# Two layers of a hybrid decoder trunk: the second block's splits at the joins pinned behind both norms, low parts issued behind four rows of blocks, and the fourth split on VectorE

## The chip, the cores and the metric

The kernel runs on one core of one Trainium2 chip. The metric is the device time of one execution in microseconds (us). TensorE (PE) multiplies matrices, VectorE (DVE), ScalarE (ACT) and GpSimd (POOL) do the elementwise work, and SyncE's queue (SP) issues the loads of the weights.

## The reference

Two layers over x of 256 tokens by 1024 features, float32. Each layer is a feed-forward block, a mixer and a second feed-forward block:

```python
def swiglu(h, w_in, w_out):
    gate, up = jnp.split(h @ w_in, 2, axis=-1)
    return (jax.nn.silu(gate) * up) @ w_out
...
for l in range(DEPTH):
    x = x + 0.5 * swiglu(rms_norm(x, norm_gain[l, 0]), w_ffn_in[l, 0], w_ffn_out[l, 0])
    x = x + hybrid_mixer(rms_norm(x, norm_gain[l, 1]), ...)
    x = x + 0.5 * swiglu(rms_norm(x, norm_gain[l, 2]), w_ffn_in[l, 1], w_ffn_out[l, 1])
```

`w_ffn_in` is 1024 by 5632 for each block, `w_ffn_out` 2816 by 1024. The mixer projects the normalised x by `w_in` (8388 columns), runs four attention branches, gates them, sums them and projects by `w_out`.

## The kernel before

**Products in two parts.** A float32 operand is split into a high part, rounded to fp32r, and a low part, the rest. `split` (L180 to L197) does this for a block of weights of 128 by 1024: ACT casts the high part `whi` (L195), then DVE, or POOL where the caller says so, subtracts it for the low part `wlo` (L196). Tile buffer numbers tell the blocks apart: `whi_5274` and `wlo_5275` are the two parts of one block. A product of 128 rows is then three matmuls, high by high, high by low, low by high: `mm3` (L199 to L202) issues the three for one block of rows (128 of the 1024 summed over) before it goes to the next.

**Blocks.** The token rows are two blocks of 128, i = 0 and 1. A feed-forward block works through pairs of column blocks j = 0 to 10. `up_first` (L268 to L297) is the product of j = 0, taken before the norm's row factors are known: 48 matmuls of 256 columns for each i (two halves g, eight rows of blocks, three parts), so 96 in all; then ACT's silu (`sl`, L283), DVE's product `av` (L285), and TensorE's transposes of `av` (L292). `up` (L299 to L324) does the other pairs with `mm2`; its first matmuls stand behind the transposes of `av` on TensorE, which takes its instructions in order.

**Splits ahead of time.** `first(j)` (L254 to L266) loads the raw weights of block j and gives four splits as things to be called later: those of j = 0 (four, low parts on POOL in the blocks behind a join) and those of j = 1, the second block (four, on DVE). The list of eight is `todo`.

**Joins.** `join` (L367 to L403) writes down the change from one block to the next: the last products of the old block, then the norm of the new one. `main(i)` of `norm` transposes x on TensorE (L140), multiplies by the gain on DVE (`xg`, L143), casts the high part `h` on ACT (L144) and subtracts the low part `h` on DVE (L147). `stats(i)` squares and sums x on ACT (`junk`, L153), adds on DVE (`ms`, L156) and takes the power on POOL (`rt`, L158). What `join` writes between `with in_order()` and its end is pinned: on TensorE, ACT and DVE those instructions keep the written order. Everything outside is placed by a scheduler that orders instructions by its own estimate of when they can start. `early` says how many splits are called ahead of the pinned part: 4 where a feed-forward block ends (its successor is a mixer or a feed-forward block), 3 where a mixer ends (its successor is a feed-forward block). Then one more split is called behind `main(0)` and one behind `main(1)`; the rest are called in `up_first` behind the first `av` (L286 to L288), outside the pinned part. The mixer's first projection (`ps0`, L527 to L535) does the same with its own list.

So there are five joins: ffn to mixer and mixer to ffn in each layer, ffn to ffn between the layers.

Of the kernel before, what the change touches and what calls it, by code (L numbers as in the profile page):

```python
# [20 lines left out]
KC = 8  # L21
# [47 lines left out]
def tile_trunk(ctx: ExitStack, tc: tile.TileContext, a: dict, out: bass.AP):  # L69
    nc = tc.nc  # L70
# [109 lines left out]
    def split(src, slots=own, eng=None):  # L180


        k, m = src.shape[1], src.shape[2]
        key = min(slots, key=lambda k: used.get(k, 0))
        ht, lt = key[:2]
        used[key] = max(used.values(), default=0) + 1
        if ht == "whi":
            hi = hi_p.tile([128, 1024], F32R, name="whi", tag="whi")
            lo = lo_p.tile([128, 1024], F32R, name="wlo", tag="wlo")
        else:  # L190
            hi = wk.tile([128, 1024], F32R, name="whi", tag=ht, bufs=NB.get(ht, 1))
            lo = wk.tile([128, 1024], F32R, name="wlo", tag=lt, bufs=NB.get(lt, 1))
        hv = hi[:, :k * m].rearrange("p (k m) -> p k m", k=k)
        lv = lo[:, :k * m].rearrange("p (k m) -> p k m", k=k)
        nc.scalar.copy(hv, src)  # L195
        (eng or nc.vector).tensor_tensor(lv, src, f(hv), op=ALU.subtract)  # L196
        return hv, lv  # L197
# [6 lines left out]
    def mm2(ps, wh, wl, r2, start, stop):  # L204
# [4 lines left out]
        for p in reversed(parts) if stop else parts:  # L209
            p()  # L210

    pinned = (mybir.EngineType.PE, mybir.EngineType.Activation, mybir.EngineType.DVE)

    @contextmanager
# [16 lines left out]
    def ffn(l, s, nxt=None, aside=None):  # L231

        early = aside is not None
# [22 lines left out]
        def first(j):  # L256

            rv, w = load_up(j), []
            slots = wide if j or not s else ends

            def one(g, q):
                w.append(split(rv[g][:, 4 * q:4 * q + 4, :], slots, nc.gpsimd if j == 0 and (l or s) else None))

            def two(c, g):
                w.append(split(rv[g][:, :, c * 128:(c + 1) * 128], slots))
            return w, [lambda x=x, y=y: (two if j else one)(x, y) for x in range(2) for y in range(2)]  # L266

        def up_first(j, w):  # L268

            for c in range(2):  # L270
                act[2 * j + c] = pair_tile()
            for i in range(NT):
                t = slice(i * 128, (i + 1) * 128)
                ps = pm.tile([128, 2, T], F32, name="pm", tag="pm")
                for g in range(2):
                    for k in range(KC):
                        wh, wl = w[2 * g + k // 4]
                        mm3(ps[:, g, :], hh[:, k, t], hl[:, k, t], wh[:, k % 4, :], wl[:, k % 4, :],
                            k == 0, k == KC - 1)
                    if i == 0:  # L280
                        yield
                sl = wk.tile([128, T], F32, name="sl", tag="sl")
                nc.scalar.activation(out=sl[:], in_=ps[:, 0, :], func=AF.Silu, scale=rs[:, i:i + 1])  # L283
                av = wk.tile([128, T], F32, name="av", tag="av")
                nc.vector.scalar_tensor_tensor(out=av[:], in0=ps[:, 1, :], scalar=rs[:, i:i + 1], in1=sl[:],  # L285
                                               op0=ALU.mult, op1=ALU.mult)  # L286
                if j == i == 0:
                    while todo:  # L288
                        todo.pop(0)()
                pst = pt.tile([128, 4, 128], F32, name="pt", tag="pt")  # L290
                for c in range(2):
                    nc.tensor.transpose(pst[:, c, :], av[:, c * 128:(c + 1) * 128], ident[:])  # L292
                for c in range(2):
                    ah, al = act[2 * j + c]
                    nc.scalar.copy(ah[:, t], pst[:, c, :])
                    nc.vector.tensor_tensor(al[:, t], pst[:, c, :], f(ah[:, t]), op=ALU.subtract)
# [77 lines left out]
    def join(rows0, grow0, tail, grow1, nxt, early):  # L374


        if nxt is None:
            rows0()
            grow0()
            for t in tail:  # L380
                t()
            grow1()
            return
        block, l, n = nxt
        todo = next(block)
        for _ in range(early):
            todo.pop(0)()
        with in_order():
            rows0()
            grow0()  # L390
            main, stats, h = norm(l, n)
            tail[0]()
            main(0)
            todo.pop(0)()
            for t in tail[1:]:
                t()
            grow1()
            block.send(h)
            main(1)
            todo.pop(0)()  # L400
            stats(0)
            next(block)
            stats(1)  # L403

    bias = const.tile([128, NLINE, T], F32, name="bias")
    gT = const.tile([128, 96], F32, name="gT")
# [75 lines left out]
    def mixer(l, nxt):  # L482
# [44 lines left out]
        hh, hl = h2[:, 0], h2[:, 1]  # L527
        ps0 = tiles()
        for i in range(NT):
            for e in range(4):  # L530
                part(ps0[i], 512, i, e, w0[e])
                if i == 0 and e % 2:
                    yield
            if i == 0:
                while todo:  # L535
                    todo.pop(0)()
# [430 lines left out]
        w = []  # L967
# [91 lines left out]
```

## Time and profile before

| | |
|---|---|
| median of 3 runs | 1365.43 us (1365.39 to 1365.67) |
| profiled execution | 1365.53 us, span 1363.8 us, so 1.73 us outside the span |
| TensorE (PE) busy | 1345.9 us, 99% |
| DVE / ACT / POOL busy | 955.2 us (70%) / 682.5 us (50%) / 352.2 us (26%) |
| mean granted clock of TensorE | 0.999 |

Rows of a timeline give the start and the duration of an instruction (or of xN like ones that follow each other), the engine, the line and the operation; in brackets stands the idle time of the engine just before it and what ended it. Successive instructions of ACT and DVE overlap a little in the rows, and those of TensorE much more, so what an instruction takes up of its engine is read from one start to the next. Idle time of TensorE is what counts here; it is 1% of the span.

### The profile page before, as it was taken

What the parts mean: (1) busy time and instruction counts of PE and PEld (TensorE: products, weight loads), DVE (VectorE), ACT (ScalarE), POOL (GpSimd) and SP (SyncE); (2) the same over time, 40 slices, a digit from 0 to 9 for tenths busy, and PEclk for the clock granted to TensorE, in tenths of its full rate; (3) what the DMA queues carried; (4) which work ended last, traced back from release to release, by engine and by line L of the source; (5) the groups of instructions that cost most, each with busy time, mean ns of one, the idle gap of its engine ahead of it and who ended that gap; (6) DMA issues with size and microseconds to landing.
All of it is one profiled execution on the core that took longest, in us unless ns stands there. A gap on an engine that the chain in (4) does not pass through costs nothing.

```text
span 1363.8 us, 20927 instructions
## 1 busy us (share of the span) xinstructions
PE 1345.9 (99%) x8129; PEld 1187.9 (87%) x8129; DVE 955.2 (70%) x1560; ACT 682.5 (50%) x1020; POOL 352.2 (26%) x296
## 2 busy tenths in 40 slices
PE   9999999999999999999999999999999999999998
PEld 8888889879999988888898888898799999888887
DVE  7767756786786677666577666567868767776663
ACT  6445435655444555444364444356554445654441
POOL 0413232240031232322413322322300212232221
PEclk9999999999999999999999999999999999999999
DMA  9589634544443475555646555354534335665530
GB/s 355 176 197 289 213 119 140 180 139 153 148 137 107 136 247 171 200 186 187 202 138 215 186 185 201 97 180 150 170 124 156 124 104 176 222 208 186 186 124 31
DMA packets 171148, 233.35 MB, mean 171 GB/s; under 512 B 5206, under 2 KB 142106, under 8 KB 171034
## 3 DMA queue, kind: packets, MB, share of 16 engines
q1 hardware_dynamic: 169724, 231.55, 52.5%
q8 instruction: 64, 1.05, 0.3%
q10 hardware_dynamic: 1326, 0.48, 0.1%
q14 instruction: 34, 0.28, 0.1%
HBM read 230.93 MB, written 1.60 MB: 171 GB/s over the span
## 4 chain that ended last, share of the span: by engine, by line
PE 93%; DVE 3%; ACT 2%; issue 1%; POOL 1%; DVEq 0%; ACTq 0%
PE pt L207 11%; PE pm L207 11%; PE pm L200 6%; PE pm L202 6%; PE pm L201 6%; PE acc L201 6%; PE acc L202 6%; PE acc L200 6%; PE pt L208 6%; PE pm L208 5%; PE zp L201 5%; PE zp L202 4%; PE zp L200 4%; PE ov L622 2%; DVE wlo L196 2%; PE pt L616 1%
## 5 line engine op out<-in xcount | busy, mean ns | idle before, releaser
L195 ACT CAST whi<-raw 128x1024 fp32r<-128x1024 f32 (+5 forms) x446 | 452.6, 1020 | 426.9 <-PE pm L201 93.8
L196 DVE TENSOR_TENSOR wlo<-raw,whi 128x1024 fp32r<-128x1024 f32 (+3 forms) x426 | 512.3, 1207 | 156.4 <-ACT whi L195 154.8
L207 PE MATMUL pt<-h,whi 128*128 128x512 f32 x640 | 231.7, 397 | 0.4
L207 PE MATMUL pm<-h,whi 128*128 128x512 f32 x640 | 231.9, 396 | 0.0
L319 POOL TENSOR_TENSOR sl<-sl,rb 128x256 f32<-128x256 f32 x80 | 91.6, 1145 | 309.8 <-ACT sl L318 309.8
L208 PE MATMUL pt<-h,wlo 128*128 128x256 f32 x640 | 166.4, 280 | 0.0
L208 PE MATMUL pm<-h,wlo 128*128 128x256 f32 x640 | 166.2, 280 | 0.0
L200 PE MATMUL pm<-h,whi 128*128 128x256 f32 x512 | 147.0, 287 | 0.4 <-DVE tg L946 0.4
L202 PE MATMUL pm<-h,wlo 128*128 128x256 f32 x512 | 146.8, 287 | 0.0
L201 PE MATMUL pm<-h,whi 128*128 128x256 f32 x512 | 146.1, 285 | 0.0
L207 PEld LDWEIGHTS pm<-h,whi 128*128 128x128 f32 x640 | 120.1, 188 | 23.0 <-issue 0.6
L207 PEld LDWEIGHTS pt<-h,whi 128*128 128x128 f32 x640 | 120.1, 188 | 22.4 <-ACT rb L166 1.0
L201 PE MATMUL acc<-wlo,act 128*128 128x512 f32 x352 | 137.9, 393 | 0.1
L202 PE MATMUL acc<-whi,act 128*128 128x512 f32 x352 | 137.5, 392 | 0.0
L200 PE MATMUL acc<-whi,act 128*128 128x512 f32 x352 | 137.1, 393 | 0.0
L323 POOL TENSOR_TENSOR act<-av,act 128x256 fp32r<-128x256 f32 x80 | 96.1, 1201 | 155.3 <-ACT act L322 155.3
L208 PEld LDWEIGHTS pt<-h,wlo 128*128 128x128 f32 x640 | 120.8, 189 | 7.1
L208 PEld LDWEIGHTS pm<-h,wlo 128*128 128x128 f32 x640 | 120.7, 189 | 6.8
L201 PE MATMUL zp<-wlo,h 128*128 128x512 f32 (+4 forms) x320 | 115.8, 362 | 1.1 <-DVE wlo L196 1.1
L202 PE MATMUL zp<-whi,h 128*128 128x512 f32 (+4 forms) x320 | 114.8, 359 | 0.0
L200 PE MATMUL zp<-whi,h 128*128 128x512 f32 (+4 forms) x320 | 109.7, 363 | 1.2 <-ACT whi L195 1.2
L200 PEld LDWEIGHTS pm<-h,whi 128*128 128x128 f32 x512 | 97.9, 191 | 3.5 <-issue 3.4
(198 smaller groups left out, 2274.9 us busy)
## 6 DMA issues: line engine op xcount, KB each, us to landing
raw<-in_w_ffn_in_dram SPq DMA_DIRECT2D x66, 1024.0 KB
raw<-in_w_in_dram SPq DMA_DIRECT2D x52, 1024.0 KB
raw<-in_w_ffn_out_dram SPq DMA_DIRECT2D x44, 1024.0 KB
raw<-in_w_ffn_in_dram SPq DMA_DIRECT2D x44, 512.0 KB
raw<-in_w_branch_dram SPq DMA_DIRECT2D x8, 1024.0 KB
raw<-in_w_out_dram SPq DMA_DIRECT2D x8, 1024.0 KB
raw<-in_w_in_dram SPq DMA_DIRECT2D x8, 768.0 KB
raw<-in_w_in_dram SPq DMA_DIRECT2D x4, 840.0 KB
```

Source lines behind the costliest of these rows:

```text
L195: nc.scalar.copy(hv, src)
L196: (eng or nc.vector).tensor_tensor(lv, src, f(hv), op=ALU.subtract)
L200: nc.tensor.matmul(ps, lhsT=lh, rhs=rh, start=start, stop=False)
L201: nc.tensor.matmul(ps, lhsT=lh, rhs=rl, start=False, stop=False)
L202: nc.tensor.matmul(ps, lhsT=ll, rhs=rh, start=False, stop=stop)
L207: parts = [lambda: nc.tensor.matmul(ps, lhsT=wh, rhs=r2, start=start, stop=stop), lambda: nc.tensor.matmul(ps[:, 0], lhsT=wl, rhs=r2[:, 0] ...
L208: lambda: nc.tensor.matmul(ps[:, 0], lhsT=wl, rhs=r2[:, 0], start=False, stop=False)]
L319: nc.gpsimd.tensor_tensor(sl[:], sl[:], rb[:], op=ALU.mult)
L323: nc.gpsimd.tensor_tensor(al, av[:], f(ah), op=ALU.subtract)
L616: nc.tensor.transpose(pst[:, c, :], ps[j][:, b * 128:(b + 1) * 128], ident[:])
L622: nc.tensor.matmul(o[:, hs[j], :], lhsT=pT[:, c, :], rhs=pv(hs[j], b), start=b == 0, stop=b == nb - 1)
```

## The change

Three edits. `mm3_late` takes four rows of blocks at a time: for each of the four high by high and high by low, and behind them the four matmuls of low by high; `up_first` and the mixer's `ps0` use it. The fourth split of j = 0 of the feed-forward blocks behind a mixer gets its low part from DVE and no longer from POOL. In `join` the split behind `main(0)` is called only where `early` is 4, and all that is left of `todo` is called behind `stats(1)`, inside the pinned part.

```diff
--- before.py
+++ after.py
@@ -209,6 +209,15 @@
         for p in reversed(parts) if stop else parts:
             p()
 
+    def mm3_late(ps, ops, start, stop):
+
+        n = len(ops)
+        for j, (lh, ll, rh, rl) in enumerate(ops):
+            nc.tensor.matmul(ps, lhsT=lh, rhs=rh, start=start and j == 0, stop=False)
+            nc.tensor.matmul(ps, lhsT=lh, rhs=rl, start=False, stop=False)
+        for j, (lh, ll, rh, rl) in enumerate(ops):
+            nc.tensor.matmul(ps, lhsT=ll, rhs=rh, start=False, stop=stop and j == n - 1)
+
     pinned = (mybir.EngineType.PE, mybir.EngineType.Activation, mybir.EngineType.DVE)
 
     @contextmanager
@@ -259,7 +268,7 @@
             slots = wide if j or not s else ends
 
             def one(g, q):
-                w.append(split(rv[g][:, 4 * q:4 * q + 4, :], slots, nc.gpsimd if j == 0 and (l or s) else None))
+                w.append(split(rv[g][:, 4 * q:4 * q + 4, :], slots, nc.gpsimd if j == 0 and (l or s) and not (s and g == q == 1) else None))
 
             def two(c, g):
                 w.append(split(rv[g][:, :, c * 128:(c + 1) * 128], slots))
@@ -273,10 +282,10 @@
                 t = slice(i * 128, (i + 1) * 128)
                 ps = pm.tile([128, 2, T], F32, name="pm", tag="pm")
                 for g in range(2):
-                    for k in range(KC):
-                        wh, wl = w[2 * g + k // 4]
-                        mm3(ps[:, g, :], hh[:, k, t], hl[:, k, t], wh[:, k % 4, :], wl[:, k % 4, :],
-                            k == 0, k == KC - 1)
+                    for q in range(2):
+                        wh, wl = w[2 * g + q]
+                        mm3_late(ps[:, g, :], [(hh[:, 4 * q + k, t], hl[:, 4 * q + k, t], wh[:, k, :], wl[:, k, :])
+                                               for k in range(4)], q == 0, q == 1)
                     if i == 0:
                         yield
                 sl = wk.tile([128, T], F32, name="sl", tag="sl")
@@ -391,7 +400,8 @@
             main, stats, h = norm(l, n)
             tail[0]()
             main(0)
-            todo.pop(0)()
+            if early == 4:
+                todo.pop(0)()
             for t in tail[1:]:
                 t()
             grow1()
@@ -401,6 +411,8 @@
             stats(0)
             next(block)
             stats(1)
+            while todo:
+                todo.pop(0)()
 
     bias = const.tile([128, NLINE, T], F32, name="bias")
     gT = const.tile([128, 96], F32, name="gT")
@@ -527,9 +539,11 @@
         hh, hl = h2[:, 0], h2[:, 1]
         ps0 = tiles()
         for i in range(NT):
-            for e in range(4):
-                part(ps0[i], 512, i, e, w0[e])
-                if i == 0 and e % 2:
+            t = slice(i * 128, (i + 1) * 128)
+            for q in range(2):
+                mm3_late(ps0[i], [(hh[:, kk, t], hl[:, kk, t], w0[kk // 2][0][:, kk % 2, :], w0[kk // 2][1][:, kk % 2, :])
+                                  for kk in range(4 * q, 4 * q + 4)], q == 0, q == 1)
+                if i == 0:
                     yield
             if i == 0:
                 while todo:
```

Three places of the order, on ACT and DVE. In the changed kernel the lines behind `mm3_late` have other numbers: the silu is L292 there, `av` L294, its transposes L301.

First, ACT at the join from mixer to ffn in layer 0, before, from the last cast of `h` to the second silu. `whi_5278` is a split of the second block, whose other three stand further ahead; `whi_5517`, `whi_5538` and `whi_5572` are splits of block j = 2, which the scheduler placed.

```order
L144 CAST h2_5189<-xg_5273 128x4x128
L195 CAST whi_5278<-raw_5142 128x1024
L153 ACTIVATE junk_5283,ss_5282<-x_87 128x512
L153 ACTIVATE junk_5285,ss_5282<-x_87 128x512
L153 ACTIVATE junk_5315,ss_5314<-x_87 128x512
L153 ACTIVATE junk_5317,ss_5314<-x_87 128x512
L195 CAST whi_5517<-raw_5512 128x1024
L283 ACT_TABLE_LOAD
L283 ACTIVATE sl_5322<-pm_5235,rt_5190 128x256
L195 CAST whi_5538<-raw_5514 128x1024
L195 CAST whi_5572<-raw_5512 128x1024
L283 ACTIVATE sl_5394<-pm_5345,rt_5190 128x256
```

ACT at the same place now, from the third of the four squares to the first silu; `whi_5318`, `whi_5322`, `whi_5326` and `whi_5330` are the second block's splits.

```order
L153 ACTIVATE junk_5311,ss_5310<-x_87 128x512
L195 CAST whi_5517<-raw_5512 128x1024
L153 ACTIVATE junk_5313,ss_5310<-x_87 128x512
L195 CAST whi_5318<-raw_5142 128x1024
L195 CAST whi_5322<-raw_5144 128x1024
L195 CAST whi_5326<-raw_5142 128x1024
L195 CAST whi_5330<-raw_5144 128x1024
L195 CAST whi_5538<-raw_5514 128x1024
L195 CAST whi_5572<-raw_5512 128x1024
L292 ACT_TABLE_LOAD
L292 ACTIVATE sl_5334<-pm_5231,rt_5190 128x256
```

Ahead of the table load and the first silu stood one split behind the squares; now six stand there. DVE at this place before, from the low part of `whi_5278` to the first `av` and one row on:

```order
L196 TENSOR_TENSOR wlo_5279<-raw_5142,whi_5278 128x1024
L156 SCALAR_TENSOR_TENSOR ms_5287<-ss_5282 128x1
L156 SCALAR_TENSOR_TENSOR ms_5319<-ss_5314 128x1
L196 TENSOR_TENSOR wlo_5518<-raw_5512,whi_5517 128x1024
L285 SCALAR_TENSOR_TENSOR av_5324<-pm_5235,rt_5190,sl_5322 128x256
L196 TENSOR_TENSOR wlo_5539<-raw_5514,whi_5538 128x1024
```

DVE at this place now, from the low part of the fourth split of j = 0 (`wlo_5275`, which was POOL's) to the first `av`:

```order
L196 TENSOR_TENSOR wlo_5275<-raw_5140,whi_5274 128x1024
L156 SCALAR_TENSOR_TENSOR ms_5283<-ss_5278 128x1
L196 TENSOR_TENSOR wlo_5518<-raw_5512,whi_5517 128x1024
L156 SCALAR_TENSOR_TENSOR ms_5315<-ss_5310 128x1
L196 TENSOR_TENSOR wlo_5319<-raw_5142,whi_5318 128x1024
L196 TENSOR_TENSOR wlo_5323<-raw_5144,whi_5322 128x1024
L196 TENSOR_TENSOR wlo_5327<-raw_5142,whi_5326 128x1024
L196 TENSOR_TENSOR wlo_5331<-raw_5144,whi_5330 128x1024
L196 TENSOR_TENSOR wlo_5539<-raw_5514,whi_5538 128x1024
L196 TENSOR_TENSOR wlo_5573<-raw_5512,whi_5572 128x1024
L294 SCALAR_TENSOR_TENSOR av_5336<-pm_5231,rt_5190,sl_5334 128x256
```

Between the second `ms` and the first `av` stood one low part; now there are six.

Second, DVE some microseconds earlier in the same join, where the low parts `h2` of the first row block are made (L147), before:

```order
L147 TENSOR_TENSOR h2_5189<-xg_5203,h2_5189 128x4x128
L196 TENSOR_TENSOR wlo_5331<-raw_5142,whi_5330 128x1024
L147 TENSOR_TENSOR h2_5189<-xg_5211,h2_5189 128x4x128
L979 TENSOR_TENSOR x_87<-xo_5047,x_87 128x512
L196 TENSOR_TENSOR wlo_5327<-raw_5144,whi_5326 128x1024
L196 TENSOR_TENSOR wlo_5335<-raw_5144,whi_5334 128x1024
L143 TENSOR_TENSOR xg_5265<-pt_5260,gn_106 128x512
```

And now:

```order
L143 TENSOR_TENSOR xg_5211<-pt_5206,gn_106 128x512
L147 TENSOR_TENSOR h2_5189<-xg_5203,h2_5189 128x4x128
L147 TENSOR_TENSOR h2_5189<-xg_5211,h2_5189 128x4x128
L993 TENSOR_TENSOR x_87<-xo_5047,x_87 128x512
L143 TENSOR_TENSOR xg_5261<-pt_5256,gn_106 128x512
L143 TENSOR_TENSOR xg_5269<-pt_5264,gn_106 128x512
```

The three low parts of the second block that stood between and behind the two rows of L147 are gone from here.

Third, DVE at the join from ffn to ffn (layer 0 to layer 1), before, from the low part of the split behind `main(1)` to the first `av`:

```order
L196 TENSOR_TENSOR wlo_7011<-raw_6870,whi_7010 128x1024
L156 SCALAR_TENSOR_TENSOR ms_7019<-ss_7014 128x1
L156 SCALAR_TENSOR_TENSOR ms_7051<-ss_7046 128x1
L196 TENSOR_TENSOR wlo_7246<-raw_7240,whi_7245 128x1024
L285 SCALAR_TENSOR_TENSOR av_7056<-pm_6967,rt_6915,sl_7054 128x256
```

And now:

```order
L196 TENSOR_TENSOR wlo_7011<-raw_6870,whi_7010 128x1024
L156 SCALAR_TENSOR_TENSOR ms_7019<-ss_7014 128x1
L156 SCALAR_TENSOR_TENSOR ms_7051<-ss_7046 128x1
L196 TENSOR_TENSOR wlo_7055<-raw_6868,whi_7054 128x1024
L196 TENSOR_TENSOR wlo_7059<-raw_6870,whi_7058 128x1024
L196 TENSOR_TENSOR wlo_7246<-raw_7240,whi_7245 128x1024
L294 SCALAR_TENSOR_TENSOR av_7064<-pm_6967,rt_6915,sl_7062 128x256
```

Two low parts of the second block, which stood ahead of the norm of the second row block (as `wlo_7059` and `wlo_7063`, by the numbers of before), now stand as `wlo_7055` and `wlo_7059` between `ms` and `av`; on ACT their casts stand in the same way between the squares and the silu.

## Rows read from the trace of the kernel before

**Rows 1.** The page: busy time of the first engines; shares of the chain.

```profile
PE 1345.9 (99%) x8129; PEld 1187.9 (87%) x8129; DVE 955.2 (70%) x1560; ACT 682.5 (50%) x1020; POOL 352.2 (26%) x296
...
PE 93%; DVE 3%; ACT 2%; issue 1%; POOL 1%; DVEq 0%; ACTq 0%
```

**Rows 2.** TensorE's waits over the span: us in total, times, longest.

```profile
PE pm L202 <- DVE h L147: 3.0, 3, 1.2
PE pt L546 <- DVE zn L559: 2.4, 2, 1.2
...
PE pt L292 <- DVE av L285: 1.0, 2, 0.5
```

**Rows 3.** Timeline of TensorE, mixer to ffn join of layer 0.

```profile
496.63 0.28 PE L200 MATMUL pm<-whi,h 128*128 128x256 f32 x1
...
499.64 0.39 PE L202 MATMUL pm<-whi,h 128*128 128x256 f32 x1 [1.19 <-DVE h L147]
...
500.93 1.03 PE L140 MATMUL pt<-ident,x 128*128 128x128 f32 x8
...
510.30 0.28 PE L202 MATMUL pm<-whi,h 128*128 128x256 f32 x1
511.11 0.41 PE L292 MATMUL pt<-ident,av 128*128 128x128 f32 x2 [0.53 <-DVE av L285]
```

**Rows 4.** Timeline of ACT, same join.

```profile
503.09 1.22 ACT L144 CAST h<-xg 128x512 fp32r<-128x512 f32 x2 [5.16 <-DVE xg L143]
504.22 1.04 ACT L195 CAST whi<-raw 128x1024 fp32r<-128x1024 f32 x1
505.17 0.62 ACT L153 ACTIVATE junk<-x 128x512 f32<-128x512 f32 x1
...
507.63 1.03 ACT L195 CAST whi<-raw 128x1024 fp32r<-128x1024 f32 x1
508.68 1.28 ACT L283 ACT_TABLE_LOAD   x1
509.97 0.47 ACT L283 ACTIVATE sl<-pm,rt 128x256 f32<-128x256 f32 x1
```

**Rows 5.** Timeline of DVE, same join.

```profile
494.97 0.69 DVE L147 TENSOR_TENSOR h<-xg,h 128x512 fp32r<-128x512 f32 x1
...
496.72 2.87 DVE L147 TENSOR_TENSOR h<-xg,h 128x512 fp32r<-128x512 f32 x1
...
505.29 1.23 DVE L196 TENSOR_TENSOR wlo<-raw,whi 128x1024 fp32r<-128x1024 f32 x1 [0.25 <-ACT whi L195]
...
510.48 0.48 DVE L285 SCALAR_TENSOR_TENSOR av<-pm,rt,sl 128x256 f32<-128x256 f32 x1 [0.56 <-ACT sl L283]
511.41 2.36 DVE L196 TENSOR_TENSOR wlo<-raw,whi 128x1024 fp32r<-128x1024 f32 x2 [0.45 <-ACT whi L195]
```

**Rows 6.** Timeline of POOL, same join.

```profile
496.56 2.48 POOL L196 TENSOR_TENSOR wlo<-raw,whi 128x1024 fp32r<-128x1024 f32 x1 [3.47 <-ACT whi L195]
```

**Rows 7.** Timeline of SP, same join: loads of raw weights.

```profile
502.48 4.43 SPq L253 DMA_DIRECT2D raw<-in_w_ffn_in_dram  x2
```

**Rows 8.** Timeline of ACT, same join: first split from those loads of w_ffn_in.

```profile
517.47 1.05 ACT L195 CAST whi<-raw 128x1024 fp32r<-128x1024 f32 x1
```

**Rows 9.** Windows at the end: length; busy time by engine; PEclk, DMA share, GB/s.

```profile
1359.00:1360.00 1.00, 0.98 (x5) 0.46 (x3) 0.68 (x1) 0.00 (x0) 0.00 (x0) 1.00 0.00 0
...
1361.00:1362.00 1.00, 0.00 (x0) 0.00 (x0) 0.00 (x0) 0.00 (x0) 0.00 (x0) 1.00 1.00 375
1362.00:1363.00 1.00, 0.00 (x0) 0.00 (x0) 0.00 (x0) 0.00 (x0) 0.00 (x0) 0.51 0.28 107
```

**Rows 10.** Timeline of TensorE at the start: matmuls ahead of the first work.

```profile
1.05 5.49 PE L103 MATMUL idle<-ones 128*128 128x128 f32 x24 [1.05 <-DVE neg_half L114]
```

**Rows 11.** Timeline of DVE, ffn to ffn join: the first av.

```profile
697.51 0.48 DVE L285 SCALAR_TENSOR_TENSOR av<-pm,rt,sl 128x256 f32<-128x256 f32 x1
```

**Rows 12.** Timeline of TensorE, same join: the transposes of av.

```profile
698.85 0.38 PE L292 MATMUL pt<-ident,av 128*128 128x128 f32 x2
```

## The prediction

> **What bounds the kernel now.** I read the page first, then TensorE's waits, then the timelines of the engines at one join. The page shows TensorE busy for 1345.9 us, 99% of the span, and the chain of waits lies on it for 93% [rows 1]. So an edit can win only from TensorE's few waits, and it can lose wherever it makes a new one. The table of waits shows which lines lose time: the low parts of `h` at L202 (3.0 us in three waits, one in the start and one in each join from mixer to ffn), a norm in the mixer (L546, 2.4 us in two) and `av` at L292 (1.0 us in two) [rows 2]. The timelines show the two that this change touches, in the join from mixer to ffn of layer 0; the join of layer 1 repeats it. TensorE begins the new block's first product at 496.63, stops for the low part of `h` and goes on at 499.64; the matmul ahead of that gap starts at 498.18 by the same timeline, so the stop costs 1.46 less a usual step of 0.12, some 1.35. At the end of the product, its last matmul starts at 510.30, and the transposes of `av` start at 511.11: 0.69 lost [rows 3]. All matmuls of the next pair stand behind those transposes.
>
> **Part 1: what the moved splits remove.** The first stop has its cause in DVE's queue. The second low part of `h` took 2.87 us where the first took 0.69 [rows 5], and it lies beside POOL's low part of the fourth split, 496.56 to 499.04 [rows 6]. With that split on DVE, and with the second block's low parts gone from between the two, L147 needs 0.69 again and ends some 2 us before TensorE wants it. The gain is 1.35 in each join. Nothing of the old block moves, so the first product still begins at 496.63, and TensorE would be through with it at 510.30 + 0.12 - 1.35 = 509.07.
>
> **Part 2: what they put in the way.** ACT and DVE take their instructions in order, and in the pinned order the second block's four splits stand behind both norms, two more from the scheduler join them, and only then come the table load, the first silu and the first `av`. When does this queue start? The transposes of the second row block stand behind the first 24 matmuls, now at 496.63 + 24 x 0.12 = 499.5 where they were at 500.93 [rows 3]; `xg` follows some 0.6 behind the start, at 500.1. Before, DVE started it at 502.38 (its casts on ACT follow at 503.09 [rows 4]), so this norm comes 2.3 earlier. ACT then does: casts of `h` from 500.8; the fourth split's cast at 504.22 - 2.3 = 501.95; the squares 0.95 later (505.17 - 504.22), which take 507.63 - 505.17 = 2.46 as before, with one cast of 0.95 among them. So the six casts begin at 501.95 + 0.95 + 2.46 + 0.95 = 506.3 [rows 4]. DVE's low part starts 1.07 behind its cast (505.29 against 504.22), at 507.4. From start to start it needs 2.36 - 1.22 = 1.14 (two of them in 2.36, of which one is 1.22) [rows 5]. Six of them: 507.4 + 6.84 = 514.2, and then `av`. ACT alone would be sooner: 506.3 + 6 x 0.95 + 1.29 for the table load = 513.3 for the silu, and `av` 0.51 behind it (510.48 against 509.97) [rows 4, 5]. DVE is therefore the later. TensorE follows 0.63 behind `av`'s start (511.11 against 510.48), at 514.85. Before it was 511.11: **+3.75 a join, +7.5 for both**. This holds both removed waits already, since both times count from the same 496.63. TensorE now stands still from 509.07 to 514.85, 5.8 us.
>
> The other instructions that move: the loads behind these splits. A raw buffer is free when both splits of it are done, so SP's two loads at 502.48 [rows 7] wait for the third and fourth low part of the queue, to about 510 and 511, and the load of `w_ffn_out` ahead of them from 499.07 to about 504.3. The first split from the loads of `w_ffn_in` was cast at 517.47 [rows 8], now some 3.7 later at 521. That is 10 us behind the issue where it was 15; two of these loads were issued within 4.43 [rows 7]. I cost them at nothing. If that cover were gone, the wait would be the part of a load beyond 10 us, in both joins.
>
> **Part 3: the ffn to ffn join.** No wait was there: `av` began at 697.51, the transposes at 698.85, as soon as the product was through [rows 11, 12]. Two low parts of 1.14 now stand ahead of `av`: 697.51 + 2.28 = 699.8, plus 0.63 = 700.4, against 698.85: **+1.55**. In the two ffn to mixer joins two splits move in the same way, but there no `av` stands behind them, and the table of waits has none of TensorE's at these joins [rows 2]: 0, with a bound of two low parts, 2.3 a join, if they were wholly bare.
>
> **Part 4: low parts behind four rows.** Low by high is wanted eight matmuls later than before, 8 x 0.12 = 0.95. At the joins this is inside part 2. In the first block of the kernel it sets against the third wait of L202 (3.0 less two of 1.2, so 0.6) [rows 2]: I take **-0.5**, between 0 and -0.95. In the mixers the scheduler puts some transposes elsewhere, around the norm that L546 waits for: 0, between -2.4, if both its waits went [rows 2], and +2.1 for both, if in each eight transposes (1.03 [rows 3]) that used to run in the wait no longer do.
>
> **Part 5: the clock.** A stop of 5.8 us on TensorE is not in the trace, outside its two ends. At the end TensorE's last matmul is over before 1360.0; the granted clock is 1.00 in the window of 1361 to 1362 and 0.51, the lower level (1.2 GHz), in the next [rows 9]. So it fell about 2 us behind the last work. In the new stop that would come at 511 to 512, and TensorE would begin the second pair at half speed. How long it stays so no row shows. The bounds: nothing, if it does not fall; and half of 5.49 us, 2.75, if it takes as long to come back as the matmuls that the kernel runs ahead of its first work [rows 10]. I take 2.0 a join, nearer the upper end, since the stop is almost three times what the clock bore at the end: **+4.0**.
>
> The Trainium skill says on this ("TensorE: Matmul & The Clock Gate", Part 1) that half rate is the array's default state, that sustained matmul activity releases it, and that the clock goes back when the engine idles. By it the slow stretch comes in each of the two joins; by the rows of work alone, where the clock never fell between two matmuls, part 5 would be 0.
>
> **Sum.** 7.5 + 1.55 - 0.5 + 4.0 = 12.55. The profiled execution took 1365.53 (span 1363.8 and 1.73 around it), 0.10 above the median: 1378.1.
>
> **The rivals.**
> *The clock stays up.* For it: in the work of this trace it never fell. Against: the stop is longer than any there. Time: 1365.53 + 8.55 = 1374.1. Chance 0.22.
> *Half the queue.* If the six splits start about 2.5 us sooner than I have it, because `xg` is not held by TensorE's 24 matmuls, or if a low part costs less with POOL quiet, `av` waits for some 1.3 beyond before, TensorE stands still for 3 us, and the clock barely matters: 2 x 1.3 + 1.0 - 0.5 = 3, so 1368.6; with two more of the six covered, 1366. Against it: 1.14 was read where POOL had nothing to do. Chance 0.12.
> *The queue is through in time, and the change wins.* Only the removed waits would count: two times 1.35 + 0.69 = -4.1, and -0.5 at the start: 1360.9. It is decided where the sixth low part ends: it has to be before 508.4, that is 0.63 ahead of TensorE's end of the product at 509.07, so the six have to start at 501.6 and not at 507.4. For it speaks only that the casts of the fourth split are ready about then; against it the order, with the squares ahead of them on ACT. Chance 0.06.
> *The change does nothing that counts*, since each new wait is won back later by a TensorE that waited there anyway. Against: the page has no other waits of this size. 1365.5, chance 0.04.
>
> **How the numbers follow.** My forecast has 0.56. Two tenths of a per cent, 2.7 us, is about what a measurement of this kernel can tell from no change. Slower by more than that are the forecast, the rival with the clock up and most of the third case: 0.86. Within it: a part of the third and the last: 0.08. Faster: 0.06. The forecast's own bounds run from 1374 (clock price 0) to 1380 (2.75 each, and the mixers' +2.1 makes 1382). The range goes down to 1368.5, to take in most of the half queue, and up to 1383, for a load that comes late.
>
> **What would show it.** Right: no wait of L202 on `h` in the two joins; a wait of TensorE of 5 to 6 us on `av`, twice; the table load on ACT near 512; `av` right behind six low parts, near 514.2; a wait of 1 to 2 us at the same line in the ffn to ffn join; matmuls of twice the duration behind the long waits, with a granted clock of 0.5 for some microseconds. Wrong: TensorE's wait on `av` below 3 us, or a long wait on a raw load.

## The result, and the profile after

The changed kernel takes 1377.68 us (median of 5 runs, 1377.2 to 1378.88), the kernel before 1365.43 on the same chip: 1.0092 times as long, 95% interval 1.0081 to 1.0103. It is slower by 12.25 us. The profiled execution took 1377.68, its span is 1375.9.

TensorE's waits in the profile after (us in total, times, longest), to be held against [rows 2]:

```profile
PE pt L301 <- DVE av L294: 12.6, 3, 5.6
PE pt L560 <- DVE zn L573: 2.2, 2, 1.1
PE pm L201 <- DVE wlo L196: 1.5, 2, 0.8
```

The wait for the low part of `h` is gone from the list. In its place stands one line of 12.6 us: three waits for `av`. The join from mixer to ffn of layer 0, on ACT, DVE and TensorE, answers to [rows 3 to 5]. ACT, timeline of the changed kernel:

```profile
506.29 5.77 ACT L195 CAST whi<-raw 128x1024 fp32r<-128x1024 f32 x6
512.08 1.28 ACT L292 ACT_TABLE_LOAD   x1
513.37 0.84 ACT L292 ACTIVATE sl<-pm,rt 128x256 f32<-128x256 f32 x2
```

DVE, same window:

```profile
494.92 1.29 DVE L147 TENSOR_TENSOR h<-xg,h 128x512 fp32r<-128x512 f32 x2
496.78 0.69 DVE L993 TENSOR_TENSOR x<-xo,x 128x512 f32<-128x512 f32 x1 [0.57 <-PE xo L202]
500.08 1.29 DVE L143 TENSOR_TENSOR xg<-pt,gn 128x512 f32<-128x512 f32 x2 [2.61 <-PE pt L140]
...
507.36 6.90 DVE L196 TENSOR_TENSOR wlo<-raw,whi 128x1024 fp32r<-128x1024 f32 x6 [0.27 <-ACT whi L195]
514.18 0.87 DVE L294 SCALAR_TENSOR_TENSOR av<-pm,rt,sl 128x256 f32<-128x256 f32 x2
```

TensorE, same window:

```profile
508.45 0.64 PE L219 MATMUL pm<-whi,h 128*128 128x256 f32 x4
514.71 0.69 PE L301 MATMUL pt<-ident,av 128*128 128x128 f32 x2 [5.62 <-DVE av L294]
515.05 0.77 PE L207 MATMUL pm<-h,whi 128*128 128x512 f32 x1
```

The two low parts of `h` take 1.29 together where the second alone took 2.87. The six casts, the table load, the six low parts and `av` follow one another, and TensorE's transposes begin at 514.71. DVE stands still for 2.61 between its add and `xg`: that is where two of the second block's low parts ran before (the third stood between the two rows of `h`). The first matmul with 512 columns behind the wait takes 0.77. Its like before (timeline of TensorE):

```profile
511.27 0.48 PE L207 MATMUL pm<-h,whi 128*128 128x512 f32 x1
```

The windows of the changed kernel (length; busy by engine; PEclk, DMA share, GB/s) say why:

```profile
513.00:514.00 1.00, 0.00 (x0) 0.00 (x0) 1.00 (x2) 0.99 (x3) 0.00 (x0) 1.00 1.06 373
514.00:515.00 1.00, 0.29 (x2) 0.29 (x3) 1.00 (x3) 1.00 (x2) 0.00 (x0) 0.58 1.08 379
515.00:516.00 1.00, 1.00 (x5) 0.90 (x4) 0.87 (x2) 0.41 (x2) 0.00 (x0) 0.50 0.90 285
516.00:517.00 1.00, 1.00 (x5) 0.80 (x4) 0.80 (x3) 0.17 (x1) 0.00 (x0) 0.50 0.99 340
517.00:518.00 1.00, 1.00 (x6) 0.86 (x5) 0.29 (x1) 0.10 (x1) 0.00 (x0) 0.72 1.12 347
518.00:519.00 1.00, 1.00 (x8) 0.92 (x7) 0.00 (x0) 0.00 (x0) 0.00 (x0) 1.00 1.01 342
```

The granted clock is at its lower level, 1.2 GHz, from about 514.2 to 517.6.

**Where the 12.2 us came in.** Both programs issue 8129 matmuls, so the n-th of one trace can be held against the n-th of the other. The difference of their starts grows from stage to stage; what each stage adds, in us:

```
start of the kernel                     -0.36
mixer of layer 0                        +0.33
join mixer to ffn, layer 0              +4.38
join ffn to ffn                         +1.58
mixer of layer 1                        +1.27
join mixer to ffn, layer 1              +4.97
sum at the last matmul                 +12.18   (1359.59 -> 1371.77)
```

### The profile page after: what moved, and what is told of

Its sections match the earlier page's. It is cut to its first block, busy times and chain, and to the rows that moved or that the text cites. A ratio compares the mean times of both kernels' runs of the same rounds, so it can differ in the third digit from the quotient of the medians.

```text
span 1375.9 us, 20928 instructions
## 1 busy us (share of the span) xinstructions
PE 1349.3 (98%) x8129; PEld 1191.7 (87%) x8129; DVE 953.9 (69%) x1562; ACT 680.8 (49%) x1020; POOL 346.0 (25%) x294
## 4 chain that ended last, share of the span: by engine, by line
PE 94%; DVE 3%; ACT 2%; issue 1%; DMA 0%; POOL 0%; SPq 0%; ACTq 0%; DVEq 0%
PE pm L207 11%; PE pt L207 11%; PE acc L200 6%; PE acc L201 6%; PE acc L202 6%; PE pm L200 6%; PE pm L208 6%; PE pt L208 5%; PE pm L201 5%; PE pm L202 5%; PE zp L201 4%; PE zp L202 4%; PE zp L200 4%; PE ov L636 2%; DVE wlo L196 2%; PE pt L630 1%
## 5 line engine op out<-in xcount | busy, mean ns | idle before, releaser
L207 PE MATMUL pm<-h,whi 128*128 128x512 f32 x640 | 234.8, 400 | 0.0
L207 PE MATMUL pt<-h,whi 128*128 128x512 f32 x640 | 231.6, 396 | 0.5 <-ACT rb L166 0.4
L200 PE MATMUL pm<-h,whi 128*128 128x256 f32 x512 | 147.0, 287 | 0.4 <-DVE tg L960 0.4
L202 PE MATMUL pm<-h,wlo 128*128 128x256 f32 x512 | 146.8, 287 | 0.0
L207 PEld LDWEIGHTS pm<-h,whi 128*128 128x128 f32 x640 | 121.6, 190 | 23.5 <-issue 0.6
L207 PEld LDWEIGHTS pt<-h,whi 128*128 128x128 f32 x640 | 120.1, 188 | 22.5 <-ACT rb L166 0.9
L202 PE MATMUL acc<-whi,act 128*128 128x512 f32 x352 | 137.5, 392 | 0.0
L200 PE MATMUL acc<-whi,act 128*128 128x512 f32 x352 | 137.2, 394 | 0.0
L201 PE MATMUL zp<-wlo,h 128*128 128x512 f32 (+4 forms) x288 | 102.8, 357 | 1.1 <-DVE wlo L196 1.1
L202 PE MATMUL zp<-whi,h 128*128 128x512 f32 (+4 forms) x288 | 102.2, 355 | 0.0
L200 PEld LDWEIGHTS pm<-h,whi 128*128 128x128 f32 x512 | 97.9, 191 | 3.5 <-issue 3.4
L320 DVE TENSOR_TENSOR z<-pt,sl 128x512 f32<-128x512 f32 x80 | 55.3, 692 | 64.5 <-POOL sl L328 62.8
```

The lines of the kernel that those rows point to most:

```text
L200: nc.tensor.matmul(ps, lhsT=lh, rhs=rh, start=start, stop=False)
L201: nc.tensor.matmul(ps, lhsT=lh, rhs=rl, start=False, stop=False)
L202: nc.tensor.matmul(ps, lhsT=ll, rhs=rh, start=False, stop=stop)
L207: parts = [lambda: nc.tensor.matmul(ps, lhsT=wh, rhs=r2, start=start, stop=stop), lambda: nc.tensor.matmul(ps[:, 0], lhsT=wl, rhs=r2[:, 0] ...
L320: nc.vector.tensor_tensor(z[:], ps[g][:], by[:].rearrange("p (o t) -> p o t", o=1) .to_broadcast([128, 2, T]), op=ALU.mult)
```

## The experiments

My theory: the low parts pinned behind both norms form one queue ahead of `av`; they leave a stretch in which DVE is free, and the stop that they make drops TensorE's clock. Rivals: one of the other two edits (the order of the low parts; POOL's split given to DVE) is the cause, or the pinning itself is, whatever the queue's length. Each ratio is to the kernel before on the same chip, whose median lay between 1365.38 and 1365.52. What a stage adds is read as in the table above, from n-th against n-th matmul of the profiled execution.

**One edit alone: the order of the low parts.** Only `mm3_late` and its two users:

```diff
-                        mm3(ps[:, g, :], hh[:, k, t], hl[:, k, t], wh[:, k % 4, :], wl[:, k % 4, :],
-                            k == 0, k == KC - 1)
+                        mm3_late(ps[:, g, :], [...], q == 0, q == 1)
```

> The kernel before with mm3_late alone. If the queue of splits ahead of av is the cause of the loss: start -0.4, mixers +0.3 and +1.3 as in the changed kernel, and nothing at the mixer to ffn joins, because the stop for the low part of h shrinks by 0.95 but av still comes at about 510.5: 1366.6 us. If the new order of the low parts is itself the cause: near 1377.

Measured: 1365.85 us, ratio 1.0004 (0.9995 to 1.0013), no difference that can be told. The stop for the low part of `h` shrinks to two of 0.5 (waits: `PE pm L219 <- DVE h L147` 1.0 in two), and TensorE then waits longer for `av` (2.5 in two), as expected: what the first wait gives, the second takes. This edit is not the cause.

**One edit alone: the pinned calls.**

```diff
             next(block)
             stats(1)
+            while todo:
+                todo.pop(0)()
```

> The kernel before with the second block's splits called behind stats(1) in the pinned part, alone. If the queue is the cause: four low parts stand between the norms and av in place of six, and the fourth split of j = 0 is out of that queue (POOL has it), so av starts at 511.0 and the transposes at 511.6 (+0.5 a join), the stop for the low part of h is gone, and the ffn to ffn join loses 1.6: 1368.0 us. If calling them there is by itself the whole cause: 1376 or more.

Measured: 1371.09 us, ratio 1.0041 (1.0028 to 1.0053). The queue was as computed (timeline of DVE):

```profile
506.32 4.63 DVE L196 TENSOR_TENSOR wlo<-raw,whi 128x1024 fp32r<-128x1024 f32 x4 [0.78 <-ACT whi L195]
510.96 0.48 DVE L285 SCALAR_TENSOR_TENSOR av<-pm,rt,sl 128x256 f32<-128x256 f32 x1
```

`av` starts at 510.96 for an expected 511.0. Most of the miss of 3 us is the clock: TensorE stood still for only 2.7 us, and yet (windows of the same run):

```profile
511.00:512.00 1.00, 0.41 (x3) 0.44 (x3) 0.55 (x2) 1.00 (x2) 0.00 (x0) 0.51 1.09 390
512.00:513.00 1.00, 1.00 (x5) 0.90 (x4) 1.00 (x1) 1.00 (x2) 0.00 (x0) 0.50 1.08 370
513.00:514.00 1.00, 1.00 (x5) 0.81 (x5) 1.00 (x2) 1.00 (x2) 0.00 (x0) 0.50 0.86 281
```

The joins cost 1.75 and 1.55 in place of 0.5, which is 2.3 of the miss, and the ffn to ffn join 1.59. So the pinned calls alone bring some 5.7 of the 12.2 us; the low part of `h` no longer waits here either, with POOL still making the fourth low part: without the second block's low parts between, it is done before POOL starts.

**One edit alone: the fourth split.** DVE in place of POOL, and no split behind `main(0)`:

```diff
-            todo.pop(0)()
+            if early == 4:
+                todo.pop(0)()
...
-... nc.gpsimd if j == 0 and (l or s) else None))
+... nc.gpsimd if j == 0 and (l or s) and not (s and g == q == 1) else None))
```

> The kernel before with the fourth split on DVE and no split behind main(0), alone; the second block's splits are where the scheduler puts them, three of them early. If the queue is the cause: two more casts (block j = 2) stand ahead of the table load, av at 511.3, transposes at 511.95, +0.85 a join: 1367.1 us. If moving the fourth split from POOL to DVE is itself the cause: near 1376. If the removed stop alone counts: 1361 to 1363.

Measured: 1366.25 us, ratio 1.0007 (0.9998 to 1.0016): +0.8 by the medians, within what can be told from no change. A wait of TensorE for the casts of the second row block (`PE pm L200 <- ACT h L144`, 1.3 in two) and one for `av` (2.5 in two) replace the removed stop. The joins add 0.5 each, for an expected 0.85.

**All but the pinned calls.** The changed kernel without the two lines behind `stats(1)`.

> The changed kernel with only the last edit undone: the second block's splits are no longer called behind stats(1) but in up_first, outside the pinned part. If the queue is the cause: as with the split alone (+0.85 a join), start -0.4, mixers +1.6, no loss at the ffn to ffn join: 1368.3 us, and the wait of TensorE on av between 1 and 3 us, with no fall of the clock at the joins. If the queue is not the cause: near 1377.

Measured: 1366.82 us, ratio 1.0010 (1.0001 to 1.0019). TensorE's waits for `av` are 3.4 in two, and the granted clock stays 1.00 behind them. So taking back these two lines takes back 10.9 of 12.25 us, while adding them alone costs 5.7: the edits work together. With the fourth split not behind `main(0)` and its low part on DVE, the queue ahead of `av` is six long (four low parts of the second block and two of block j = 2) and not four (three and one). The joins add 0.5 and 0.4 here, the mixers 0.3 each, and the start nothing (-0.05); the expectation had 0.85, 1.6 for both mixers, and -0.4.

**The clock by itself.** Matmuls that only keep TensorE at work, ahead of the first transposes of `av`:

```diff
                 pst = pt.tile([128, 4, 128], F32, name="pt", tag="pt")
+                if j == i == 0 and s:
+                    for _ in range(25):
+                        nc.tensor.matmul(pst[:, 0, :], lhsT=ones[:], rhs=ones[:], start=True, stop=True)
```

> The changed kernel with 25 extra matmuls (128 by 128, results overwritten) on TensorE ahead of the first transposes of av at the two mixer to ffn joins, 25 x 0.229 = 5.7 us, so the transposes start at about 514.7 as in the changed kernel, but TensorE has worked all the time. If the clock's fall costs time: granted clock 1.00 behind the wait and 1377.7 - 1.5 - 2.1 = 1374.1 us. If it does not: 1377.7.

Measured: 1373.68 us, ratio 1.0058 (1.0044 to 1.0072). The windows of this run show 1.00 throughout the work:

```profile
514.00:515.00 1.00, 1.00 (x11) 1.00 (x10) 0.98 (x2) 0.67 (x1) 0.00 (x0) 1.00 1.03 326
515.00:516.00 1.00, 1.00 (x8) 0.87 (x7) 1.00 (x2) 0.85 (x3) 0.00 (x0) 1.00 0.98 326
```

Useless work on TensorE makes the kernel 4.0 us faster than the change. But more than the clock is different here (timelines of TensorE and of DVE):

```profile
502.09 3.73 PE L302 MATMUL pt<-ones 128*128 128x128 f32 x32
511.38 0.48 DVE L294 SCALAR_TENSOR_TENSOR av<-pm,rt,sl 128x256 f32<-128x256 f32 x1
```

The scheduler put the fillers into the middle of the product, from 502.1 to about 509, and block j = 2 behind the silu. So `av` is ready at 511.9, the product ends late instead, and the transposes start at 514.74. Up to the transposes the two joins add 3.3 each, near the change's 3.7 and 3.6. Behind them this run gains some 0.4 in each join where the change loses another 0.8 and 1.3. These differences, 1.2 and 1.8, are what this run has to say on the price of the clock. The rest of the 4.0 is the mixer of layer 1, which kept its clock (1.0 less), against a start that is 0.3 later.

**The mixer's projection as before.** The changed kernel with `ps0` in the old order.

> The changed kernel with the mixer's first projection in the order of before (low by high straight behind each block of rows); up_first keeps the new order. If the mixers' loss (0.3 and 1.3 by the two traces) comes from that edit: 1376.1 us, no fall of the clock near 968. If it is chance or comes from elsewhere: 1377.7.

Measured: 1378.28 us, ratio 1.0092 (1.0078 to 1.0106). The time did not fall to 1376.1, and both mixers still lose 0.3. The run with the pinned calls alone, where `ps0` was never touched, shows the same 0.3 in both. So the new order in `ps0` is not needed for that loss. The total hides a trade: layer 1's mixer kept its clock and added 0.9 less than in the change, while the start and the two joins, whose stops are as long as in the change (5.62), came out 0.5, 0.5 and 0.7 higher.

**`av` first.** One split ahead of the first silu, one between the two, all others behind (joins from mixer to ffn; the other joins and `ps0` as before):

```diff
             stats(1)
-            while todo:
-                todo.pop(0)()
+            if early == 3:
+                todo.pop(0)()
...
+                with in_order(pinned[1:] if s and j == 0 else ()):
                     sl = ...
                     av = ...
+                    if s and j == 0:
+                        while len(todo) > (2 if i == 0 else 0):
+                            todo.pop(0)()
```

and block j = 2's casts tied behind the last of these.

> The changed kernel with one split of the second block ahead of the first silu, one between the first av and the second silu, the last two and those of block j = 2 behind the second silu, at the mixer to ffn joins; the splits of the ffn to ffn join and the mixer's projection as before. If the queue ahead of av is the cause, av starts near 508 and TensorE never waits for it: the transposes near 509.1 where they were at 511.1, 2.0 saved a join, less some 0.2 for the next split, and -0.4 at the start: 1361.3 us. If something else of the change costs the time: 1366 or more.

Measured: 1373.93 us, ratio 1.0063 (1.0051 to 1.0076): a clear miss. Two lines of the waits say where:

```profile
PE acc L201 <- DVE wlo L196: 4.2, 2, 2.1
PE acc L200 <- ACT whi L195: 2.6, 2, 1.3
```

The low parts that were put behind `av` came back some 8 us later, as the splits of `w_ffn_out` that the first `acc` products need. The joins add 3.0 and 4.4. And `av` was not as early as I had it (timeline of ACT):

```profile
505.86 1.03 ACT L195 CAST whi<-raw 128x1024 fp32r<-128x1024 f32 x1
508.37 1.28 ACT L293 ACT_TABLE_LOAD   x1 [1.49 <-PE pm L219]
509.67 0.47 ACT L293 ACTIVATE sl<-pm,rt 128x256 f32<-128x256 f32 x1
```

The table load waits for TensorE here, for the product of the first row block. That product ends late: the fourth split's low part ends at 504.7 (POOL's ended at 499.0 [rows 6]), and matmuls of the second row block stand ahead. Another 1.0 is the mixer of layer 0, where the clock fell (window of this run), though `ps0` and the joins in front of the mixers are as in the kernel before:

```profile
288.00:289.00 1.00, 1.00 (x5) 1.00 (x5) 1.00 (x3) 1.00 (x3) 0.00 (x0) 0.50 0.99 350
```

So it is not enough to shorten the queue ahead of `av`; DVE's free time has to be used.

**DVE's free time.** The changed kernel with two splits of the second block called while DVE stands still:

```diff
             main(0)
-            if early == 4:
-                todo.pop(0)()
+            todo.pop(0 if early == 4 else 1)()
             for t in tail[1:]:
                 t()
             grow1()
+            if early == 3:
+                todo.pop(1)()
```

> The changed kernel with two of the second block's splits called earlier in the pinned part of the mixer to ffn joins: one behind main(0), one behind grow1, where DVE stands still. If the cost is DVE's free time given away: the low parts fill that gap, the norm of the second row block is not later, four low parts in place of six stand ahead of av, which starts at 511.9 and not at 514.2; 2.2 less a join, and some 0.6 less for the clock, which still falls: 1372.7 us. If the low parts only push later ones back, or the pinning itself costs: 1377.

Measured: 1375.54 us, ratio 1.0067 (1.0055 to 1.0080), with a wide spread, 1371.69 to 1376.32. At the joins the expectation held: `xg` of the second row block is not later (500.97, in a run that is 0.9 behind by then), four low parts stand ahead of `av`, TensorE's stop is 3.6 and not 5.8 (2.2 less), and the joins add 2.1 and 2.2 in place of 4.4 and 5.0. The profiled run is still 1.9 above the expected 1372.7. Of this 1.0 came from the mixers: each added 1.3, with the clock down in both. Another 1.1 lies behind the last matmul, which starts 5.3 before the end of the span and 4.1 before it in the change. The window in layer 1:

```profile
968.00:969.00 1.00, 1.00 (x4) 1.00 (x4) 0.88 (x4) 0.70 (x2) 0.44 (x1) 0.50 0.39 137
```

**The queue fitted to the free time.** All of it at the joins from mixer to ffn, the other joins and `ps0` as before:

```diff
             main(0)
-            if early == 4:
-                todo.pop(0)()
+            todo.pop(0)()
+            if early == 3:
+                stats(0)
...
             grow1()
+            if early == 3:
+                todo.pop(0)()
+                todo.pop(1)()
             block.send(h)
             main(1)
             todo.pop(0)()
-            stats(0)
+            if early == 4:
+                stats(0)
             next(block)
             stats(1)
-            while todo:
+            if early == 3:
                 todo.pop(0)()
```

The second block's splits are kept by their place (`w[2 * c + g]`), and the casts of block j = 2 are tied behind the first silu.

> At the mixer to ffn joins: the fourth split (on DVE) behind main(0) again, two splits of the second block behind grow1, one behind main(1), one behind stats(1), stats(0) already behind main(0), block j = 2 held behind the first silu; ffn to ffn join and mixer projection as before. If the loss is low parts ahead of av and DVE's free time: no stop for the low part of h, the first row block's product done at 503, av near 508 and the transposes at 509.1 where they were at 511.1, no new waits behind it: -2.0 a join, -0.4 at the start, +0.3 to +0.6 in the mixers: 1361.5 us. If, as in the run before it with av first, the splits put off come back as waits of the acc products: 1366 or more.

Measured: **1361.58 us**, ratio 0.9972 (0.9960 to 0.9983) to the kernel before: 3.9 us faster than before, 16.1 faster than the change. DVE, timeline of this run:

```profile
496.34 1.23 DVE L196 TENSOR_TENSOR wlo<-raw,whi 128x1024 fp32r<-128x1024 f32 x1 [0.26 <-ACT whi L195]
497.58 0.16 DVE L156 SCALAR_TENSOR_TENSOR ms<-ss 128x1 f32<-128x1 f32 x1
497.65 0.69 DVE L1003 TENSOR_TENSOR x<-xo,x 128x512 f32<-128x512 f32 x1
498.52 2.36 DVE L196 TENSOR_TENSOR wlo<-raw,whi 128x1024 fp32r<-128x1024 f32 x2 [0.18 <-ACT whi L195]
500.80 1.28 DVE L143 TENSOR_TENSOR xg<-pt,gn 128x512 f32<-128x512 f32 x2
...
505.90 1.23 DVE L196 TENSOR_TENSOR wlo<-raw,whi 128x1024 fp32r<-128x1024 f32 x1 [0.78 <-ACT whi L195]
507.69 0.48 DVE L296 SCALAR_TENSOR_TENSOR av<-pm,rt,sl 128x256 f32<-128x256 f32 x1 [0.56 <-ACT sl L292]
```

DVE works with no gap over 0.3 through the stretch in which it stood still, `av` is 6.5 sooner than in the change, and TensorE goes from the product into the transposes without a wait (timeline):

```profile
508.32 0.65 PE L219 MATMUL pm<-whi,h 128*128 128x256 f32 x4
508.81 0.38 PE L303 MATMUL pt<-ident,av 128*128 128x128 f32 x2
```

What is left is a wait of 0.6 for the second `av`. Five splits are pinned at each of these joins, as many as in the change, so pinning by itself is not what costs the time. Which of the moves in this run is worth how much, no run separates.

**Which join costs what.** The pinned calls at the joins from mixer to ffn alone:

```diff
-            while todo:
+            while early == 3 and todo:
                 todo.pop(0)()
```

> The changed kernel with the pinned calls behind stats(1) at the two mixer to ffn joins alone; the ffn to ffn and the ffn to mixer joins leave the rest of the list to the scheduler, as before. If the ffn to ffn join cost 1.6 for its two low parts ahead of av: that wait is gone there and L1 begins 1.6 sooner; and if the pinned calls at the ffn to mixer joins made the mixers' +0.3 and +1.3 (with the clock's fall there), these go too: 1377.7 - 1.6 - 0.3 - 1.3 = 1374.5 us. If the two mixer to ffn joins are the whole loss: 1377.7. The waits on av there stay at 5.8 each.

Measured: 1376.37 us, ratio 1.0077 (1.0064 to 1.0091). The ffn to ffn join adds nothing now (5.21 before it, 5.22 behind it, n-th against n-th matmul), so its 1.6 belongs to the two low parts ahead of `av` there. Layer 1's mixer kept its clock. Its wait at the norm is back at 0.45, as in the kernel before, but a later wait (L200 on `tg`, 0.5 for 0.2) adds 0.3 all the same. Layer 0's 0.3 stayed, so the pinned calls at the ffn to mixer joins are not needed for that one. Over all runs, the longer wait at the norm (0.76 for 0.45) stands in layer 0 wherever either the pinned calls at the ffn to mixer joins or the new order in `ps0` is there, and in layer 1 only with those pinned calls. The two joins added 4.9 and 4.8.

## Why the prediction was right, point by point

**Part 1, the removed stop: right.** The two low parts of `h` also take 1.28 together in the run of the fourth split alone, where POOL is quiet, and the second alone takes 2.89 where only the order of the low parts changed and POOL works beside it; this bears out POOL's low part beside it as the cause. In the change the wait of L202 is gone, and the product's last four matmuls end the work of TensorE at about 508.9, for 509.07 forecast.

**Part 2, the queue: right in mechanism and size.** Casts from 506.29 (forecast 506.3), low parts from 507.36 (507.4), `av` at 514.18 (514.2), transposes at 514.71 (514.85): +3.60 for +3.75. DVE was the later of the two engines, as computed, though by little: ACT's silu at 513.37 would have let `av` begin near 513.9. The loads went as forecast too: SP's pair was issued at 510.88, and no wait on a raw tile appears at this join:

```profile
510.88 1.50 SPq L262 DMA_DIRECT2D raw<-in_w_ffn_in_dram  x2
```

**Part 3, ffn to ffn: right.** +1.58 for +1.55. The timelines of DVE and of TensorE there, against [rows 11, 12]:

```profile
700.72 3.50 DVE L196 TENSOR_TENSOR wlo<-raw,whi 128x1024 fp32r<-128x1024 f32 x3 [0.78 <-ACT whi L195]
704.13 0.48 DVE L294 SCALAR_TENSOR_TENSOR av<-pm,rt,sl 128x256 f32<-128x256 f32 x1
```

```profile
704.76 0.41 PE L301 MATMUL pt<-ident,av 128*128 128x128 f32 x2 [1.36 <-DVE av L294]
```

**Part 4, low parts: the start right in number only, the mixers mis-sized.** The start gave -0.36 for -0.5, but that is luck. The wait of 0.57 for the low part of `h` is gone, and the new order gains 0.6 with it in the first block; by 50 us this is lost again, 0.4 of it in a new wait (`PE pt L207 <- ACT rb L166`). What is left comes from the matmuls that the kernel runs ahead of its first work; in this execution they took 5.08 for 5.49 [rows 10]:

```profile
1.05 5.08 PE L103 MATMUL idle<-ones 128*128 128x128 f32 x24 [1.05 <-DVE neg_half L114]
```

In the five runs with the new order in which these matmuls end as in the kernel before, the start comes to between -0.18 and +0.11. In the two runs without the new order, where they end up to 0.3 sooner, it comes to -0.40 and -0.22. So of the forecast 0.5 at most 0.2 lasted.

The mixers were put at 0 within -2.4 and +2.1; they gave +0.33 and +1.27. The scheduler moved transposes out of a wait near the norm, which grew by 0.3 in each. TensorE in layer 1, before and after:

```profile
959.17 0.50 PE L201 MATMUL pm<-wlo,cks 128*128 128x512 f32 x1 [0.45 <-DVE wlo L196]
965.37 0.50 PE L201 MATMUL pm<-wlo,cks 128*128 128x512 f32 x1 [0.76 <-DVE wlo L196]
```

In layer 1 the clock fell besides, which is the other 1.0 (windows after):

```profile
968.00:969.00 1.00, 1.00 (x5) 0.84 (x6) 0.91 (x3) 1.00 (x3) 0.00 (x0) 0.56 1.08 384
969.00:970.00 1.00, 1.00 (x4) 1.00 (x4) 0.98 (x4) 1.00 (x2) 0.07 (x1) 0.50 0.76 266
970.00:971.00 1.00, 1.00 (x4) 1.00 (x4) 0.72 (x2) 0.05 (x2) 1.00 (x1) 0.50 0.00 0
```

In layer 0, with the same waits, it stayed at 1.00, so this 1.0 is not a fixed price of the change.

**Part 5, the clock: right in kind, 2.0 a join against 1.3 and 1.9.** These are what the changed kernel loses from the transposes at 514.71 until its clock is back at about 517.6, and from those at 1196.1 until 1200.2, n-th against n-th matmul. The fall did not come at 511 to 512 as forecast: in layer 0 it came some 5 us into the stop, at about 514.2, in layer 1 some 3 us into it. The rule of the Trainium skill that the prediction named ("TensorE: Matmul & The Clock Gate", Part 1: half rate is the default, activity releases it, idling brings it back) agrees with these rows, and with the run with filler matmuls, where TensorE had no stop at the joins and the clock stayed at 1.00.

**What offset what.** The joins were forecast at 5.75 each and came to 4.38 and 4.97. Both got back some 0.5 behind the wait that I had not counted: before, TensorE lost a little at the matmuls with `dg` (L165, at 520), and after the long wait these are spread among the others. The 2.2 us too much there and the 1.6 too little in the mixers nearly cancel, and 1.0 of that 1.6 is the clock's fall in one mixer. That the total is within 0.5 us is partly luck.

**The rivals.** "The clock stays up" fell by the windows. "Half the queue" fell by the rows above. "The queue is through in time" named the right point: in the fitted kernel the last low part ahead of `av` ends at 507.1, ahead of the 508.4 that the prediction gave, and the kernel does win: 1361.6, for the 1360.9 of that rival. "The change does nothing that counts" fell by the result: the new waits were not won back.

## What to carry to other kernels

A write-up order that pins work "behind" something is also a queue ahead of whatever comes next on that engine: count the instructions that stand between the norm and the one result that the bottleneck waits for, on each engine, at their start-to-start price. Before moving work, look for where the engine stands still and waits for the bottleneck; work taken out of such a stretch costs its full time later, and moving it still further back only changes the line on which TensorE waits. A stop of the bottleneck is to be priced with its clock: here a stop of 5.8 us cost 1.3 and 1.9 more in slow matmuls.

## What the runs showed of the hardware that was not expected

What the clock does behind a stop differs from one execution to the next. Behind a stop of 1.9 us (all but the pinned calls) the granted clock stayed at 1.00; behind one of 2.7 (pinned calls alone) it was 0.5 for three windows. The stop at the mixer to ffn joins was equally long (5.62) in the changed kernel, in the run with the old `ps0` and in the one with the pinned calls at these joins alone; the joins added 4.4 and 5.0, 4.9 and 5.7, and 4.9 and 4.8.

The clock also falls without one long stop. In the mixer, waits of 0.8 and 1.1 us with 1.4 us of matmuls between them were followed by 0.5 in layer 1 of the changed kernel and in both layers of the run that used DVE's free time. The same waits left it at 1.00 in layer 0 of the changed kernel and in both layers of the runs with the old `ps0`, with the pinned calls alone and with the fillers. And in layer 0 of the run with `av` first it fell behind waits of 0.45 and 1.21, which are those of the kernel before, where it stayed at 1.00. So the fall in the mixer does not need the change's longer waits.

That makes times of such kernels vary: 1371.69 us at a mean granted clock of 0.999 and 1376.32 us at 0.993 for one and the same kernel (the one that used DVE's free time), where the fitted kernel spread over 1.2 us. What decides it in a given execution no run here shows.
